# Sliding windows on one core: both windows of one channel half in one copy

## The chip, the cores and the metric

The kernel runs on one core of a Trainium2 chip. The metric is the device time of one execution in microseconds, as the median of several runs.

## The reference

The input is 16 images of 64 channels and 64 x 64 float32 values. Every 8 x 8 window at stride 4 is copied out, 15 x 15 of them an image. Nothing is computed; 16.8 MB are read and 62.9 MB are written.

```python
n_h = (h - window_size) // stride + 1
n_w = (w - window_size) // stride + 1
for i in range(n_h):
    for j in range(n_w):
        result[:, i, j] = x[:, :, i*stride : i*stride + 8, j*stride : j*stride + 8]
```

## The kernel before

**Layout.** Lt holds the whole input in SBUF. A partition is (channel half, image, quarter of the image's rows): 2 x 16 x 4 = 128 partitions, each with 32 channels of 16 rows of 64 values. So partitions 0 to 63 hold the first half of the channels and 64 to 127 the second. A channel takes 1024 values and 32 of padding (PAD). Windows that begin at row 0 or 4 or 8 of a quarter lie within one partition; those that begin at row 12 need the first four rows of the next quarter, which lies on the next partition.

**Output.** One window of one image has 4096 values (16 KB), in the order channel, row, column. A row of windows (15 of them) is cut into 10 lines of 6144 values (24 KB): a line is three halves of a window, numbered n = 0, 1, 2. One half of a window is the 32 channels of one channel half. In a line the channel halves alternate, so n = 0 and n = 2 are of the same channel half in two neighbouring windows, and n = 1 is of the other. `line(k)` lists the three for line k.

**Buffers.** GG has room for three tiles of 24 KB a partition. At the start it is also the staging place for part of the input: the loads at L126 (on the ACT and SP queues) bring some channels there, the copies at L145 move them into Lt, and the loads at L61 (SP and POOL queues) bring the rest directly. The tiles are handed out in a ring: tile t may be filled when the scatter of the tile that had the place before has landed.

**Tiles, in program order.**

- part(y, j), six of them: 16 KB a partition, whole windows for half of the images (y), with four copies of 32 partitions for each channel half (L196), on ACT and DVE by turns. The first three are filled in places of 16 KB, so that a later tile of 24 KB can lie over two of them; and a tile of 24 KB that follows a part tile finds its third n free early.
- plain(k), for k = 4 to 8: a line for windows that begin at rows 0 and 4 of the quarters, rows 0 on the one half of the partitions and rows 4 on the other. Six copies of 64 partitions x 2048 values: three on ACT (L216), and on DVE one written as a shuffle with an identity mask (L154) and two copies (L216).
- cross(k), ten of them: a line for windows that begin at rows 8 and 12. Rows 8 are three copies on ACT (L229). Rows 12 are made on DVE of three shuffles (L154), which bring four rows from the next partition, and three copies (L233), 64 x 1024 values each. Of 128 partitions 16 have no window; their rows' indices are out of bounds and the scatter drops them.
- two edge tiles for the last line of a row: 64 partitions, with copies split over channels between ACT (12 channels) and DVE (20) at L260, and a plain store on the SP queue (L261).

plain(4) to plain(6) alternate with the last three part tiles. Then comes plain(7), cross(0) to cross(4), plain(8), cross(5) to cross(9), and the edges.

**Stores.** All but the edge tiles go out through `scatter` (L162): an indirect DMA issued by POOL, which writes each partition's run to the row of the output that an index tile names (idx for plain, idx_y0 or idx_y1 for part, idx_hi or idx_lo for cross). The index tiles are made once at the start by 21 small operations on DVE. The stores are declared to write rows of their own, so none waits for another. The framework schedules the copies of each engine; only the moves and the part copies keep program order.

## Time and profile before

| | |
|---|---|
| median of 3 runs | 185.22 us (185.2 to 185.27) |
| the profiled execution | 184.96 us, of it 183.2 us span |
| DVE busy | 142.1 us, 183 instructions |
| ACT busy | 140.8 us, 82 instructions |
| POOL busy | 40.0 us, 42 instructions |
| HBM read, written | 16.78 MB, 62.91 MB |

The span runs from the first to the last instruction of the program on the core. A group of instructions is given as line, engine, operation, output <- input, shape and count, then busy us and mean ns of one, then the engine's idle time just before them and what ended it. "DMA out_dram<-GG,idx" as the one that ended an idle time is the landing of a scatter whose tile's place is then free. A queue's share is the time of its packets as a share of 16 DMA engines' span.

### The profile page before, as it was taken

To read this page: it belongs to the slowest core of one execution; us is meant where nothing else is said; L and a number is where in the kernel's file an instruction comes from. 1 tells how busy PE (TensorE), PEld (TensorE's weight loads), DVE (VectorE), ACT (ScalarE), POOL (GpSimd) and SP (SyncE) were. 2 spreads that over 40 slices of the span, in tenths; PEclk is the share of its full clock that TensorE was granted. 3 is DMA by queue.
4 is the path that set the end of the run, shared out by engine and by line. 5 is a ranking of instruction groups with operands and counts; after the bars stand their busy time and mean duration, and the time that the engine had idled before them with its cause. 6 is when DMAs were issued, how large, how long until landed. Compare 5 with 4: busy or idle time off the path is not lost.

```text
span 183.2 us, 516 instructions
## 1 busy us (share of the span) xinstructions
DVE 142.1 (78%) x183; ACT 140.8 (77%) x82; POOL 40.0 (22%) x42
## 2 busy tenths in 40 slices
DVE  4002998999999959979999588979879689986900
ACT  0002998999999969989899488979979789987900
POOL 7500754033330420231112202201220220230000
DMA  4999999999999999999999999999999999999994
GB/s 154 397 413 410 410 410 411 411 412 437 426 440 456 429 395 440 438 429 433 429 453 429 429 431 429 429 435 429 429 429 435 429 431 419 429 429 435 429 429 182
DMA packets 9509, 75.80 MB, mean 414 GB/s; under 512 B 2753, under 2 KB 2753, under 8 KB 6849
## 3 DMA queue, kind: packets, MB, share of 16 engines
q0 software_dynamic: 6736, 62.92, 81.1%
q1 hardware_dynamic: 2192, 10.75, 14.3%
q10 hardware_dynamic: 576, 2.10, 3.1%
q14 instruction: 5, 0.03, 0.0%
HBM read 16.78 MB, written 62.91 MB: 435 GB/s over the span
## 4 chain that ended last, share of the span: by engine, by line
DMA 75%; DVE 11%; POOL 3%; ACT 2%; issue 2%; ACTq 0%; DVEq 0%; PEldq 0%
DMA out_dram<-GG,idx 28%; DMA out_dram<-GG,idx_lo 21%; DMA Lt<-in_x_dram 20%; DVE GG L154 7%; DMA out_dram<-GG,idx_hi 6%; POOL Lt L61 3%; ACT GG L260 2%; DVE GG L233 2%; DVE GG L196 2%; DVE GG L216 1%; ACTq L292 0%; DVEq L154 0%; POOL pi L77 0%; DVEq L216 0%; PEldq L292 0%
## 5 line engine op out<-in xcount | busy, mean ns | idle before, releaser
L229 ACT COPY GG<-Lt 64x2048 f32<-64x2048 f32 x30 | 56.9, 1897 | 9.4 <-DMA out_dram<-GG,idx 4.9
L154 DVE STREAM_SHUFFLE GG<-Lt 64x1024 f32<-64x1024 f32 (+1 forms) x35 | 50.5, 1443 | 0.9
L196 DVE COPY GG<-Lt 32x2048 f32<-32x2048 f32 x30 | 36.6, 1218 | 4.4 <-DMA out_dram<-GG,idx 2.9
L196 ACT COPY GG<-Lt 32x2048 f32<-32x2048 f32 x18 | 34.1, 1897 | 3.0 <-DMA out_dram<-GG,idx 2.1
L216 ACT COPY GG<-Lt 64x2048 f32<-64x2048 f32 x15 | 28.3, 1897 | 1.5 <-DMA out_dram<-GG,idx_lo 1.3
L145 DVE COPY Lt<-GG 32x2048 f32<-32x2048 f32 (+1 forms) x10 | 11.3, 1172 | 13.6 <-DMA GG<-in_x_dram 13.5
L233 DVE COPY GG<-Lt 64x1024 f32<-64x1024 f32 x30 | 20.5, 683 | 0.6
L61 POOL DMA_DIRECT2D Lt<-in_x_dram x16 | 13.9, 878 | 15.8 <-DMA Lt<-in_x_dram 15.3
L162 POOL DMA_INDIRECT out_dram<-GG,idx_y x6 | 9.4, 1573 | 31.5 <-DVE GG L196 27.2
L145 ACT ACT_TABLE_LOAD x1 | 1.3, 1283 | 17.0 <-DMA GG<-in_x_dram 17.0
L216 DVE COPY GG<-Lt 64x2048 f32<-64x2048 f32 x10 | 12.1, 1221 | 0.2
L260 ACT COPY GG<-Lt 32x768 f32<-32x768 f32 x12 | 10.0, 830 | 2.1 <-DMA out_dram<-GG,idx_lo 1.3
L260 DVE COPY GG<-Lt 32x1280 f32<-32x1280 f32 x12 | 9.8, 819 | 2.1 <-DMA out_dram<-GG,idx_lo 1.3
L162 POOL DMA_INDIRECT out_dram<-GG,idx_lo x5 | 4.8, 960 | 29.8 <-DVE GG L233 29.8
L162 POOL DMA_INDIRECT out_dram<-GG,idx_hi x5 | 5.3, 1066 | 26.2 <-DVE GG L233 18.0
L162 POOL DMA_INDIRECT out_dram<-GG,idx x5 | 6.3, 1252 | 20.2 <-ACT GG L216 17.1
L145 ACT COPY Lt<-GG 32x2048 f32<-32x2048 f32 (+1 forms) x6 | 10.3, 1752 | 0.1
L154 DVE LOAD_MASK_SELECT GG<-Lt x35 | 0.3, 8 | 8.7 <-DMA out_dram<-GG,idx 3.8
L80 DVE TENSOR_SCALAR tb<-pi 128x1 int32<-128x1 int32 x1 | 0.2, 154 | 1.0 <-POOL pi L77 1.0
L83 DVE TENSOR_SCALAR tb<-tb 128x1 int32<-128x1 int32 x2 | 0.3, 153 | 0.0
L86 DVE TENSOR_TENSOR th<-tc,tq 128x1 int32<-128x1 int32 x2 | 0.3, 150 | 0.0
L77 POOL IOTA pi<- 128x1 int32 x1 | 0.1, 124 | 0.4 <-PEq L292 0.4
(20 smaller groups left out, 2.9 us busy)
## 6 DMA issues: line engine op xcount, KB each, us to landing
Lt<-in_x_dram POOLq DMA_DIRECT2D x8, 800.0 KB, 16.4
out_dram<-GG SPq DMA_DIRECT2D x2, 1536.0 KB
Lt<-in_x_dram SPq DMA_DIRECT2D x6, 384.0 KB
GG<-in_x_dram ACTq DMA_DIRECT2D x4, 512.0 KB
Lt<-in_x_dram SPq DMA_DIRECT2D x6, 320.0 KB
GG<-in_x_dram SPq DMA_DIRECT2D x4, 448.0 KB
Lt<-in_x_dram SPq DMA_DIRECT2D x2, 704.0 KB
Lt<-in_x_dram POOLq DMA_DIRECT2D x8, 64.0 KB, 16.1
```

The costliest lines, as they stand in the source:

```text
L61: eng.dma_start(out=L[p0 : p0 + QP - HQ + 1 : HQ, c0:c1, :, :], in_=x_v[ch, y, q, :, c0:c1, :])
L80: nc.vector.tensor_scalar(out=d[:, :], in0=pi[:, :], scalar1=shift, scalar2=mask, op0=ALU.logical_shift_right, op1=ALU.bitwise_and)
L83: nc.vector.tensor_scalar(out=d[:, :], in0=a[:, :], scalar1=float(m), scalar2=None, op0=ALU.mult)
L86: nc.vector.tensor_tensor(out=d[:, :], in0=a[:, :], in1=b[:, :], op=op)
L145: tc.keep_in_program_order(copy(out=L[d, c:e, :, :], in_=S[ch][f, c:e]))
L154: nc.vector.stream_shuffle(out=out, in_=in_, mask=mask)
L162: st = nc.gpsimd.indirect_dma_start(out=rows, out_offset=bass.IndirectOffsetOnAxis(ap=ix[:, 0:1], axis=0), in_=g, in_offset=None, element_ ...
L196: (act if n % 3 == 0 else dve)(out=g[d * QP : (d + 1) * QP, ch], in_=L[f : f + QP, :, s * ST : s * ST + WS, cols],)
L216: (copy or (dve if m else shf))(out=g[d, n], in_=L[f, :, half * ST : half * ST + WS, cols])
L229: act(out=g[lo, n], in_=L[f, :, s * ST : s * ST + WS, cols])
L233: dve(out=g[hi, n, :, 0:ST], in_=L[f, :, (s + 1) * ST : RB, cols])
L260: copy(out=g[d, n, c0:c1], in_=L[f, c0:c1, s * ST : s * ST + WS, cols])
```

## The change

In a line, n = 0 and n = 2 are moved by one operation, whose source pattern has one more step (two windows, 4 values apart) and whose destination is two runs of 2048 values with one such run left out between them; n = 1 has an operation of its own. `line(k)` now returns these two groups, and `windows` builds the source pattern. In plain tiles ACT takes the pair of the one row half and the single one of the other, DVE the other two. In cross and edge tiles each engine does what it did, in pairs. Part tiles keep their copies. The index tiles are made in 18 operations; idx_y1 is gone, and the second half of the images is reached by a constant offset of the scatter.

```diff
-    pi, tb, tq, tc_, th, tu, idx, idx_y0, idx_y1, idx_lo, idx_hi = (
+    pi, tb, tq, tc_, te, tu, idx, idx_y, idx_lo, idx_hi = (
...
-    tt(idx_y0, tu, th, ALU.add)
-    nc.vector.tensor_scalar(out=idx_y1[:, :], in0=idx_y0[:, :], scalar1=float(YB * NWIN), scalar2=None, op0=ALU.add)
+    tt(idx_y, tu, tq, ALU.add)
+    far(tb, te, HP + HQ - 1)
+    tt(idx_hi, idx, tb, ALU.add)
+    far(te, te, HQ - 1)
+    line_of(tc_, tc_, -2 * NR, NR)
+    tt(te, te, tc_, ALU.add)
+    tt(idx_lo, idx, te, ALU.add)
...
-        scatter(t, (idx_y0, idx_y1)[y], o_v, j)
+        scatter(t, idx_y, o_v, j + y * YB * NWIN)
...
     def line(k):
-        return [(n, (3 * k + n) % CH, slice((3 * k + n) // CH * ST, (3 * k + n) // CH * ST + WS)) for n in range(3)]
+        j, ch = 3 * k // CH, 3 * k % CH
+        return (j, ch, slice(0, 3, 2), 2), (j + ch, 1 - ch, slice(1, 2), 1)
+
+    def windows(f, c, r, j, m):
+        v = L[f, c, r, j * ST : j * ST + WS]
+        return bass.AP(tensor=v.tensor, offset=v.offset, ap=[v.ap[0], [ST, m], *v.ap[1:]])
...
     def plain(k):
         t = tile_()
         g = halves(t, 3)
-        work = [(half, n, ch, cols) for half in range(CH) for n, ch, cols in line(k)]
-        for copy, ops in ((act, work[::2]), (None, work[1::2])):
-            for m, (half, n, ch, cols) in enumerate(ops):
+        for half in range(CH):
+            for j, ch, n, m in line(k):
                 f = slice(ch * HP, (ch + 1) * HP)
                 d = slice(half * HP, (half + 1) * HP)
-                (copy or (dve if m else shf))(out=g[d, n], in_=L[f, :, half * ST : half * ST + WS, cols])
+                copy = (shf if m == 1 else act) if half == 0 else (dve if m == 2 else act)
+                copy(out=g[d, n], in_=windows(f, every, slice(half * ST, half * ST + WS), j, m))
         scatter(t, idx, o_l, k)
...
-        for n, ch, cols in line(k):
+        for j, ch, n, m in line(k):
             f = slice(ch * HP, (ch + 1) * HP)
-            act(out=g[lo, n], in_=L[f, :, s * ST : s * ST + WS, cols])
-            shf(out=g[hi, n, :, ST:WS], in_=L[f, :, 0:ST, cols], mask=nxt)
-        for n, ch, cols in line(k):
+            act(out=g[lo, n], in_=windows(f, every, slice(s * ST, s * ST + WS), j, m))
+            shf(out=g[hi, n, :, ST:WS], in_=windows(f, every, slice(0, ST), j, m), mask=nxt)
+        for j, ch, n, m in line(k):
             f = slice(ch * HP, (ch + 1) * HP)
-            dve(out=g[hi, n, :, 0:ST], in_=L[f, :, (s + 1) * ST : RB, cols])
+            dve(out=g[hi, n, :, 0:ST], in_=windows(f, every, slice((s + 1) * ST, RB), j, m))
...
-        for n, ch, cols in line(NR - 1):
+        for j, ch, n, m in line(NR - 1):
...
                 for c0, c1, copy in ((0, ACT_C, act), (ACT_C, CL, dve)):
-                    copy(out=g[d, n, c0:c1], in_=L[f, c0:c1, s * ST : s * ST + WS, cols])
+                    copy(out=g[d, n, c0:c1], in_=windows(f, slice(c0, c1), slice(s * ST, s * ST + WS), j, m))
```

More of the change, by code (lines that the diff above doesn't have):

```diff
@@ L66, in itile @@
         return ipool.tile([P, 1], i32, name=name)
-    pi, tb, tq, tc_, th, tu, idx, idx_y0, idx_y1, idx_lo, idx_hi = (
-        itile(n) for n in ("pi", "tb", "tq", "tc", "th", "tu", "idx", "idx_y0", "idx_y1", "idx_lo", "idx_hi")
+    pi, tb, tq, tc_, te, tu, idx, idx_y, idx_lo, idx_hi = (
+        itile(n) for n in ("pi", "tb", "tq", "tc", "te", "tu", "idx", "idx_y", "idx_lo", "idx_hi")
     )
@@ L86, in tt, with line_of, far @@
         nc.vector.tensor_tensor(out=d[:, :], in0=a[:, :], in1=b[:, :], op=op)
+    def line_of(d, a, mult, add):
+        nc.vector.tensor_scalar(out=d[:, :], in0=a[:, :], scalar1=float(mult), scalar2=float(add), op0=ALU.mult, op1=ALU.add)
+    def far(d, a, value):
+        nc.vector.tensor_scalar(out=d[:, :], in0=a[:, :], scalar1=float(value), scalar2=FAR, op0=ALU.is_equal, op1=ALU.mult)
     bits(tb, 2, B - 1)
-    bits(tq, 0, HQ - 1)
+    nc.vector.tensor_scalar(out=tq[:, :], in0=pi[:, :], scalar1=2, scalar2=NSLOT * (HQ - 1), op0=ALU.logical_shift_left, op1=ALU.bitwise_and)
     bits(tc_, 6, 1)
+    bits(te, 0, HP + HQ - 1)
     mul(tb, tb, NH)
-    mul(th, tq, NSLOT)
-    tt(tb, tb, th, ALU.add)
+    tt(tb, tb, tq, ALU.add)
     tt(tu, tb, tc_, ALU.add)
     mul(idx, tu, NR)
-    bits(th, 5, 1)
-    mul(th, th, 1 - YB * NWIN)
+    bits(tq, 5, 1)
+    mul(tq, tq, 1 - YB * NWIN)
     mul(tu, tu, NW)
-    tt(idx_y0, tu, th, ALU.add)
-    nc.vector.tensor_scalar(out=idx_y1[:, :], in0=idx_y0[:, :], scalar1=float(YB * NWIN), scalar2=None, op0=ALU.add)
-    nc.vector.tensor_scalar(out=tq[:, :], in0=tq[:, :], scalar1=float(HQ - 1), scalar2=FAR, op0=ALU.is_equal, op1=ALU.mult)
-    tt(th, tc_, tq, ALU.mult)
-    tt(idx_hi, idx, th, ALU.add)
-    nc.vector.tensor_scalar(out=tc_[:, :], in0=tc_[:, :], scalar1=-1.0, scalar2=1.0, op0=ALU.mult, op1=ALU.add)
-    tt(tb, tb, tc_, ALU.add)
-    mul(tb, tb, NR)
-    tt(th, tc_, tq, ALU.mult)
-    tt(idx_lo, tb, th, ALU.add)
+    tt(idx_y, tu, tq, ALU.add)
[5 more added lines that the diff above has]
+    tt(idx_lo, idx, te, ALU.add)
     NG = 3
@@ L200, in part @@
             )
-        scatter(t, (idx_y0, idx_y1)[y], o_v, j)
+        scatter(t, idx_y, o_v, j + y * YB * NWIN)
     def line(k):
-        return [(n, (3 * k + n) % CH, slice((3 * k + n) // CH * ST, (3 * k + n) // CH * ST + WS)) for n in range(3)]
+        j, ch = 3 * k // CH, 3 * k % CH
[3 more added lines that the diff above has]
+        return bass.AP(tensor=v.tensor, offset=v.offset, ap=[v.ap[0], [ST, m], *v.ap[1:]])
+    every = slice(0, CL)
     crossed = 0
```

## The prediction

> **What bounds the kernel now.** I read the page's header, its slices and its queues first, then busy time by stage, then the groups of instructions by shape, then the waits, and last the order of time on VectorE (DVE), ScalarE (ACT) and GpSimd (POOL) where one tile hands over to the next.

> ```profile
> span 183.2 us, 516 instructions
> DVE 142.1 (78%) x183; ACT 140.8 (77%) x82; POOL 40.0 (22%) x42
> DMA  4999999999999999999999999999999999999994
> q0 software_dynamic: 6736, 62.92, 81.1%
> q1 hardware_dynamic: 2192, 10.75, 14.3%
> q10 hardware_dynamic: 576, 2.10, 3.1%
> HBM read 16.78 MB, written 62.91 MB: 435 GB/s over the span
> ```

> The three DMA queues together took 81.1 + 14.3 + 3.1 = 98.5% of 16 engines' span. Only the first and the last of 40 slices are not full. DVE and ACT have 41 us each in which they do nothing. The stages say the same more closely (columns: window, its length, busy time of DVE, ACT and POOL, clock, DMA share, GB/s):

> ```profile
> 1.00:2.00 1.00, 0.96 (x11) 0.00 (x0) 0.51 (x1) 1.00 0.00 0
> 2.00:3.00 1.00, 0.86 (x9) 0.00 (x0) 1.00 (x3) 1.00 0.71 127
> 44.00:92.00 48.00, 44.01 (x40) 44.66 (x25) 11.22 (x9) 1.00 1.01 432
> 92.00:162.00 70.00, 60.26 (x90) 59.90 (x32) 9.77 (x11) 1.00 1.01 432
> 64.00:68.00 4.00, 2.09 (x2) 2.53 (x2) 0.96 (x1) 1.00 0.92 395
> 180.00:181.00 1.00, 0.00 (x0) 0.00 (x0) 0.00 (x0) 1.00 0.63 270
> ```

> The first bytes move between 2.0 and 2.3 us (0.71 of a microsecond is filled), the last in about 180.6. Between them the share is 1.0 or over in both long stages and the rate is 432 GB/s in both, although DVE and ACT are 92% busy in the one (44.01 of 48) and 86% in the other. A rate that does not follow how busy the engines are is the rate of the transfers themselves. The weakest stretch in them is 64 to 68, at 0.92: 4 x 0.08 = 0.3 us of traffic lost at most. So the kernel is a stream of transfers with about 2 us ahead of it and 2.6 us behind its last bytes, and a copy on DVE or ACT counts only where it leaves that stream without work.

> How far off that is, the scatters show:

> ```profile
> DMA to landing us min/median/max: 9.9/12.5/15.0
> 59.66 1.85 POOL L162 DMA_INDIRECT out_dram<-GG,idx_y  x1 [4.40 <-DVE GG L196]
> 65.89 0.96 POOL L162 DMA_INDIRECT out_dram<-GG,idx  x1 [4.38 <-ACT GG L216]
> 78.96 1.54 POOL L162 DMA_INDIRECT out_dram<-GG,idx  x1 [3.66 <-ACT GG L216]
> 86.14 0.96 POOL L162 DMA_INDIRECT out_dram<-GG,idx_y  x1 [5.63 <-DVE GG L196]
> 91.20 0.96 POOL L162 DMA_INDIRECT out_dram<-GG,idx  x1 [4.11 <-ACT GG L216]
> 91.29 9.59 ACT L229 COPY GG<-Lt 64x2048 f32<-64x2048 f32 x5 [0.77 <-DMA out_dram<-GG,idx]
> 98.00 12.46 DMA out_dram<-GG,idx_lo
> ```

> A line tile is 128 rows of 24 KB, 3.15 MB, or 7.3 us at 432 GB/s; a part tile is 2.10 MB, 4.9 us; a cross tile drops 16 rows, 2.75 MB, 6.4 us. From issue to landing a scatter takes 9.9 to 15.0 us, so it always waits behind another. The shortest cover is at plain(6): issued at 78.96, and the ACT copy at 91.29 is let go by its landing. Of these 12.3 us, 7.3 are its own traffic, 1.54 POOL's work on it, and about 1.5 the way from an issue to the first bytes (my estimate, from the load issues that begin at 0.74, row below, to the first bytes by 2.3). That leaves 2.0 us of waiting behind other traffic, less the receipt, for which the rows give only a bound: 183.2 - 181 = 2.2 us at the end of the kernel. The real cover there is thus between nothing and 2.0 us. For cross(0), 12.46 - 6.4 - 0.96 - 1.5 = 3.6 us, less the same receipt. I take the middle: 1 us at the tightest hand-over, and 3.6 - 1.1 = 2.5 us in the cross stage.

> ```profile
> 0.74 2.61 ACTq L126 DMA_DIRECT2D GG<-in_x_dram  x4
> ```

> **The change, part by part.** The rows for its costs:

> ```profile
> L229 ACT COPY GG<-Lt 64x2048 f32<-64x2048 f32 x30 | 56.9, 1897 | 9.4 <-DMA out_dram<-GG,idx 4.9
> L154 DVE STREAM_SHUFFLE GG<-Lt 64x1024 f32<-64x1024 f32 x30 | 38.4, 1280 | 0.7
> L233 DVE COPY GG<-Lt 64x1024 f32<-64x1024 f32 x30 | 20.5, 683 | 0.6
> L154 DVE STREAM_SHUFFLE GG<-Lt 64x2048 f32<-64x2048 f32 x5 | 12.1, 2427 | 0.2
> L216 DVE COPY GG<-Lt 64x2048 f32<-64x2048 f32 x10 | 12.1, 1221 | 0.2
> L260 ACT COPY GG<-Lt 32x768 f32<-32x768 f32 x12 | 10.0, 830 | 2.1 <-DMA out_dram<-GG,idx_lo 1.3
> L260 DVE COPY GG<-Lt 32x1280 f32<-32x1280 f32 x12 | 9.8, 819 | 2.1 <-DMA out_dram<-GG,idx_lo 1.3
> L145 ACT COPY Lt<-GG 32x1024 f32<-32x1024 f32 x1 | 1.0, 1036 | 0.0
> L145 DVE COPY Lt<-GG 32x2048 f32<-32x2048 f32 x9 | 10.7, 1227 | 13.6 <-DMA GG<-in_x_dram 13.5
> ```

> Durations. ACT: 2048 elements in 1897 ns and 1024 in 1036 make 0.841 ns an element and 175 ns of fixed cost, so one of 4096 is 3.62 us. DVE copy: 1221 and 683 ns make 0.525 ns an element and 146 fixed, so 4096 is 2.30 us. The merged shuffle of a cross tile is 64x2048, which a row has: 2.43 us in place of 2 x 1.28.

> Plain tiles (5). ACT had 3 copies, 5.7 us; it gets one of 4096 and one of 2048, 5.5. DVE had a shuffle and two copies, 2.43 + 2 x 1.22 = 4.9; it gets a shuffle and one copy of 4096, 4.7. The split between the engines stays; each tile is ready 0.2 us sooner.

> Cross tiles (10). ACT as above, 5.7 to 5.5 us. DVE: 3 x 1.28 + 3 x 0.68 = 5.9 becomes 2.43 + 1.28 + 1.22 + 0.68 = 5.6.

> Edge tiles (2). Six operations an engine become four. ACT: 6 x 0.83 = 5.0; two of 1536 elements at 1.47 and two of 768 at 0.83 make 4.6. DVE: 6 x 0.82 = 4.9; two of 2560 at 1.49 and two of 1280 at 0.82 make 4.6.

> Sum of busy time. ACT loses 5 + 10 + 4 = 19 operations of 175 ns, 3.3 us. DVE loses 5 + 10 + 4 = 19 copies of 146 ns and 10 shuffles of 133 (2 x 1280 - 2427), 4.1 us. All of it lies beside transfers: the share is 1.0 wherever these copies run. On the path it is worth nothing. If the cover were gone, it would be worth at most 5 x 0.2 + 10 x 0.3 + 2 x 0.3 = 4.6 us, which is also what the change would have brought to a kernel bound by its copies.

> What is no longer done early. This is the one place where the change takes something away. A line tile that takes a buffer after a part tile (16 of 24 KB) had its third window column, n = 2, free before the rest. The order on DVE shows such pieces run ahead of their tile:

> ```profile
> 63.89 1.22 DVE L216 COPY GG<-Lt 64x2048 f32<-64x2048 f32 x1
> 85.40 1.29 DVE L154 STREAM_SHUFFLE GG<-Lt 64x1024 f32<-64x1024 f32 x1
> 90.34 0.69 DVE L233 COPY GG<-Lt 64x1024 f32<-64x1024 f32 x1
> 79.16 6.21 DVE L196 COPY GG<-Lt 32x2048 f32<-32x2048 f32 x5 [0.97 <-DMA out_dram<-GG,idx]
> ```

> The 64x1024 shuffle at 85.40 and the copy at 90.34 belong to a cross tile, while plain(7) is still being filled (its scatter goes out at 91.20). An operation over n = 0 and n = 2 must wait for both. For plain(6), plain(7) and cross(1) up to one ACT copy (1.90 us) and 1.2 to 2.0 us of DVE then move behind the landing. But the pieces run ahead stood in front of the tile that was due: without them plain(5) and plain(7) go out 1.2 to 2.0 us sooner. In this stage tiles wait for engines more than for landings (DVE 44.01 of 48 us busy), so for plain(6) and plain(7) it cancels. Only cross(1) comes later, by about 1.3 us, behind cross(0), whose traffic still fills 6.4 us. Cost on the path: nothing; bounds 0 and +1.3 - 1 = +0.3 us if the cover there is as thin as at plain(6).

> Waits. Each merged operation waits for all the landings that its two halves waited for. Behind it on ACT stands the other copy of the tile, on DVE the rest of it, and the scatter on POOL waits for both. The two halves of an operation lie on either side of n = 1, which the other engine writes in a plain tile; if the two were ordered one after the other, ACT's 3.62 and then DVE's 2.43 make 6.05 against 5.74 now: +0.3 a tile, within the cover.

> Index tiles. 3 of 21 operations on 128x1 go, 0.15 us each:

> ```profile
> L101 DVE TENSOR_SCALAR idx_y<-idx_y 128x1 int32<-128x1 int32 x1 | 0.2, 154 | 0.0
> ```

> 0.45 us of DVE at the start, on an engine that next waits 13.5 us for the staged loads (L145's row above). Nothing. idx_y1 goes because the second half of the batch is now a constant offset of the scatter; rows and bytes stay.

> Descriptors. No DMA is added or moved past another. But POOL's work on a scatter depends on what DVE runs beside it: 0.96 us at 86.14 beside shuffles, 1.85 at 59.66 beside 1.22 us copies. The second has 0.89 us more than the first, 0.73 of such a copy. The copy beside it in a plain tile will be one of 2.30 us. The bounds are 0.96 (never in its way) and 0.96 + 2.30 = 3.3 us (a whole copy), so -0.9 to +1.4 against the 1.85 of now, at the three part scatters that go out beside plain copies (59.66, 73.98, 86.14); I take the same share of the longer copy, 0.96 + 0.73 x 2.30 = 2.6 us, +0.8, and it is covered: even the shortest flight, 9.9 us, has 9.9 - 4.9 - 0.96 - 1.5 = 2.5 us behind other traffic, less the receipt. [...]

> **Sum.** 0 on the path. The profiled execution took 184.96 us, 1.8 around a span of 183.2; the median of the runs is 185.22, 0.26 above it. 184.96 + 0 + 0.26 = 185.2 us.

> **Rivals.** What this kernel's measurement can tell from no change is about 0.2%, 0.37 us.

> A, slower: late descriptors. POOL's longer wait beside the longer copies costs the stream its cover in the part stage. It decides once a scatter is late by more than the cover of 1 us: +1.4 at each of three, less 1, is +0.4 a tile, +1.2 in all: 186.4. For: 1.85 against 0.96, and the part stage has DVE 92% busy. Against: a part scatter has 2.5 us behind other traffic where plain(6) has 2.0, and plain(6)'s 1.54 passed without a dip. Chance 0.12.

> B, slower: DVE loses half its rate on the new pattern. [...] Against: L145 keeps the full rate (1227 ns) with a stride in both operands. Chance 0.05. [...]

> C, slower: order. A merged 3.62 us copy placed ahead of a tile that is due delays it by 1.7 us more than a single one; less 1, +0.7: 185.9. Chance 0.03.

> D, faster. The 0.3 us of dip at 64 to 68, and others as small, close because tiles come 0.2 to 1.2 us sooner: 184.7. Against: at 64 to 68 the scatter issued at 59.66 was already waiting, so lateness is not what made it. Chance 0.10.

> E, the merged operations are taken apart again when the program is lowered: counts as now, 185.2. It lies within no change.

> **The numbers.** No change, E included, 0.70; A, B and C make slower 0.20; D faster 0.10. The range goes from D, 184.7, to A, 186.4, and leaves out B and part of D, under 1 in 10 with the far ends of A.

> **What would show it.** Right: 19 fewer ACT copies, 15 of them 64x4096 at 3.6 us; 5 DVE copies of 64x4096 at 2.3; 15 shuffles of 64x2048 and 10 of 64x1024; both engines 3 to 4 us less busy and idle for longer behind landings; 432 GB/s from 44 to 162. Wrong: a DMA share under 0.92 in any 4 us between 44 and 176, POOL over 2.5 us on a scatter, a DVE copy near 4.7 us, or a span that moves by over 0.4 us with the stream still full.

## The result and the profile after

The changed kernel takes 184.71 us in the median of 14 runs (184.51 to 185.06); the kernel before took 185.15 us in 14 runs beside it (184.97 to 185.27). The ratio is 0.9977 [0.997, 0.9984], so 0.44 us or 0.23% less. That is within the range of 184.7 to 186.4, but just past the 0.2% that the forecast of "no change" allowed, on the side that it gave a chance of 0.1. The profiled execution took 184.68 us, 1.8 around a span of 182.9.

The page's header and queues after, with the line that names the fourth queue, which the prediction did not weigh:

```profile
span 182.9 us, 453 instructions
DVE 138.7 (76%) x141; ACT 137.5 (75%) x63; POOL 40.4 (22%) x42
DMA  4999999999999999999999999999999999999995
q0 software_dynamic: 6736, 62.92, 81.3%
q1 hardware_dynamic: 2192, 10.75, 14.3%
q10 hardware_dynamic: 576, 2.10, 3.1%
q14 instruction: 3, 0.02, 0.0%
HBM read 16.78 MB, written 62.91 MB: 436 GB/s over the span
```

The fourth queue in the kernel before:

```profile
q14 instruction: 5, 0.03, 0.0%
```

DVE has lost 3.4 us and ACT 3.3 (142.1 and 140.8 before). POOL has 0.4 more. The queues take 81.3 + 14.3 + 3.1 = 98.7% of the span where they took 98.5%: the same traffic in a span that is 0.3 us shorter. The stages of the changed kernel (columns as before):

```profile
44.00:92.00 48.00, 41.61 (x33) 42.22 (x20) 10.93 (x9) 1.00 1.01 432
92.00:162.00 70.00, 60.62 (x63) 60.14 (x23) 9.69 (x11) 1.00 1.01 431
64.00:68.00 4.00, 1.57 (x2) 2.30 (x2) 0.96 (x1) 1.00 0.92 395
180.00:181.00 1.00, 0.00 (x0) 0.00 (x0) 0.00 (x0) 1.00 0.52 221
181.00:182.00 1.00, 0.00 (x0) 0.00 (x0) 0.00 (x0) 1.00 0.01 0
```

The rate is what it was, 432 and 431 GB/s against 432 twice. The dip from 64 to 68 is there unchanged, 0.92 and 395 GB/s. Nothing in the stream has become denser. Only the end differs: from 180 to 181 a share of 0.52 where there was 0.63. This view counts a packet's whole time where the packet starts. The packet records show when the last one ends: at 181.89 us before and at 181.61 after. So the last bytes do not stop at about 180.6, as the prediction read the view, and 1.3 us of the span lie behind them in both kernels, not 2.6. Its forecast does not hang on this.

The groups by shape, the merged operations first:

```profile
L238 ACT COPY GG<-Lt 64x4096 f32<-64x4096 f32 x10 | 36.0, 3603 | 8.4 <-DMA out_dram<-GG,idx_lo 4.6 <-DMA out_dram<-GG,idx 3.3 <-DMA out_dram<-GG,idx_hi 0.3
L225 ACT COPY GG<-Lt 64x4096 f32<-64x4096 f32 x5 | 18.0, 3604 | 3.7 <-DMA out_dram<-GG,idx_y 2.1 <-DMA out_dram<-GG,idx_lo 1.5
L225 DVE COPY GG<-Lt 64x4096 f32<-64x4096 f32 x5 | 11.4, 2289 | 0.2
L155 DVE STREAM_SHUFFLE GG<-Lt 64x2048 f32<-64x2048 f32 x15 | 36.4, 2428 | 0.3
L155 DVE STREAM_SHUFFLE GG<-Lt 64x1024 f32<-64x1024 f32 x10 | 12.8, 1280 | 0.3
L269 ACT COPY GG<-Lt 32x1536 f32<-32x1536 f32 x4 | 5.9, 1469 | 2.6 <-DMA out_dram<-GG,idx_lo 2.4 <-DMA out_dram<-GG,idx_hi 0.2
L269 DVE COPY GG<-Lt 32x2560 f32<-32x2560 f32 x4 | 5.9, 1486 | 2.4 <-DMA out_dram<-GG,idx_lo 2.3
```

15 ACT copies of 64x4096 at 3603 and 3604 ns (3.62 us was worked out), 5 on DVE at 2289 (2.30), 15 shuffles of 64x2048 at 2428 (2.43), and the edge copies at 1469 and 1486 (1.47 and 1.49). So the copies did what the prediction said.

The scatters that the prediction named (start, length, what ended POOL's idle time):

```profile
48.62 2.39 POOL L163 DMA_INDIRECT out_dram<-GG,idx_y  x1 [4.36 <-DVE GG L197]
59.64 0.97 POOL L163 DMA_INDIRECT out_dram<-GG,idx_y  x1 [4.40 <-DVE GG L197]
74.08 0.96 POOL L163 DMA_INDIRECT out_dram<-GG,idx_y  x1 [7.43 <-DVE GG L197]
78.88 1.69 POOL L163 DMA_INDIRECT out_dram<-GG,idx  x1 [3.84 <-ACT GG L225]
86.19 0.96 POOL L163 DMA_INDIRECT out_dram<-GG,idx_y  x1 [5.63 <-DVE GG L197]
103.54 0.96 POOL L163 DMA_INDIRECT out_dram<-GG,idx_hi  x1 [4.74 <-issue]
162.47 2.39 POOL L163 DMA_INDIRECT out_dram<-GG,idx_hi  x1 [6.05 <-ACT GG L238]
```

### The profile page after: what moved, and what is told of

Its sections match the earlier page's. It is cut to its first block, busy times and chain, and to the rows that moved or that the text cites. A ratio compares the mean times of both kernels' runs of the same rounds, so it can differ in the third digit from the quotient of the medians.

```text
span 182.9 us, 453 instructions
## 1 busy us (share of the span) xinstructions
DVE 138.7 (76%) x141; ACT 137.5 (75%) x63; POOL 40.4 (22%) x42
## 3 DMA queue, kind: packets, MB, share of 16 engines
q0 software_dynamic: 6736, 62.92, 81.3%
q1 hardware_dynamic: 2192, 10.75, 14.3%
HBM read 16.78 MB, written 62.91 MB: 436 GB/s over the span
## 4 chain that ended last, share of the span: by engine, by line
DMA 75%; DVE 13%; POOL 3%; issue 2%; DVEq 1%; POOLq 0%; PEldq 0%
DMA out_dram<-GG,idx 28%; DMA out_dram<-GG,idx_lo 21%; DMA Lt<-in_x_dram 20%; DMA out_dram<-GG,idx_hi 6%; DVE GG L155 6%; POOL Lt L61 3%; DVE GG L242 2%; DVE GG L197 2%; DVE GG L269 2%; DVE GG L225 1%; DVEq L301 1%; POOL pi L77 0%; DVEq L155 0%; POOLq L163 0%; DVEq L269 0%
## 5 line engine op out<-in xcount | busy, mean ns | idle before, releaser
L238 ACT COPY GG<-Lt 64x4096 f32<-64x4096 f32 (+1 forms) x20 | 55.0, 2750 | 8.6 <-DMA out_dram<-GG,idx_lo 4.6
L155 DVE STREAM_SHUFFLE GG<-Lt 64x2048 f32<-64x2048 f32 (+1 forms) x25 | 49.2, 1969 | 0.6
L197 ACT COPY GG<-Lt 32x2048 f32<-32x2048 f32 x18 | 34.1, 1897 | 4.0 <-DMA out_dram<-GG,idx 2.8
L225 ACT COPY GG<-Lt 64x4096 f32<-64x4096 f32 (+1 forms) x10 | 27.5, 2750 | 3.8 <-DMA out_dram<-GG,idx_y 2.1
L242 DVE COPY GG<-Lt 64x2048 f32<-64x2048 f32 (+1 forms) x20 | 19.1, 955 | 0.5
L163 POOL DMA_INDIRECT out_dram<-GG,idx_y x6 | 8.8, 1474 | 31.8 <-DVE GG L197 31.8
L163 POOL DMA_INDIRECT out_dram<-GG,idx_hi x5 | 6.2, 1248 | 28.7 <-DVE GG L242 17.9
L225 DVE COPY GG<-Lt 64x4096 f32<-64x4096 f32 x5 | 11.4, 2289 | 0.2
L269 ACT COPY GG<-Lt 32x1536 f32<-32x1536 f32 (+1 forms) x8 | 9.2, 1150 | 2.7 <-DMA out_dram<-GG,idx_lo 2.4
L269 DVE COPY GG<-Lt 32x2560 f32<-32x2560 f32 (+1 forms) x8 | 9.2, 1152 | 2.5 <-DMA out_dram<-GG,idx_lo 2.3
L163 POOL DMA_INDIRECT out_dram<-GG,idx x5 | 6.4, 1283 | 20.5 <-ACT GG L225 18.2
```

Of the source, the lines that this page charges most:

```text
L155: nc.vector.stream_shuffle(out=out, in_=in_, mask=mask)
L163: st = nc.gpsimd.indirect_dma_start(out=rows, out_offset=bass.IndirectOffsetOnAxis(ap=ix[:, 0:1], axis=0), in_=g, in_offset=None, element_ ...
L197: (act if n % 3 == 0 else dve)(out=g[d * QP : (d + 1) * QP, ch], in_=L[f : f + QP, :, s * ST : s * ST + WS, cols],)
L225: copy(out=g[d, n], in_=windows(f, every, slice(half * ST, half * ST + WS), j, m))
L238: act(out=g[lo, n], in_=windows(f, every, slice(s * ST, s * ST + WS), j, m))
L242: dve(out=g[hi, n, :, 0:ST], in_=windows(f, every, slice((s + 1) * ST, RB), j, m))
```

## The experiments

Each edit is against the kernel before, or against the changed one where it says so. Each kernel was run 5 to 12 times beside 24 to 33 runs of the kernel before, whose median was 185.09 to 185.13 us; differences are against that median.

### One part at a time

**Index tiles alone.** The kernel before, with the 18 index operations of the change and the constant offset in the scatter; the copies stay single.

```diff
-    pi, tb, tq, tc_, th, tu, idx, idx_y0, idx_y1, idx_lo, idx_hi = (
+    pi, tb, tq, tc_, te, tu, idx, idx_y, idx_lo, idx_hi = (
...
-        scatter(t, (idx_y0, idx_y1)[y], o_v, j)
+        scatter(t, idx_y, o_v, j + y * YB * NWIN)
```

> The kernel before with only the index tiles in 18 operations and idx_y with the constant offset. Theory F (the stream of transfers is full from 2 to 180 us; only what its two ends look like can count): 0.0 us, as DVE waits 13.5 us for the staged loads after them; at most -0.1 us. Theory I (fewer small operations and a shorter program at the start let the first loads move sooner): -0.3 to -0.4 us, the whole gain.

The result, -0.33 us, is the number of theory I, but its mechanism did not show: the first packet starts at 2.18 us with and without the edit.

**Copies alone.** All merged copies, with the 21 index operations of before.

```diff
-            act(out=g[lo, n], in_=L[f, :, s * ST : s * ST + WS, cols])
+            act(out=g[lo, n], in_=windows(f, every, slice(s * ST, s * ST + WS), j, m))
...
-                    copy(out=g[d, n, c0:c1], in_=L[f, c0:c1, s * ST : s * ST + WS, cols])
+                    copy(out=g[d, n, c0:c1], in_=windows(f, slice(c0, c1), slice(s * ST, s * ST + WS), j, m))
```

> The changed kernel with the 21 index operations of before: all the merged copies and nothing else. Theory F: -0.3 to -0.45 us, the whole gain, all of it after 143 us. Theory I: 0.0 us.

**Edges alone** has only the second of these two edits (the edge tiles), **lines alone** only the first with its like in plain and cross.

> Only the two edge tiles have merged copies; all else as before. Theory E (the gain is the tail: the edge stores go out sooner, and the last packets end more evenly): -0.3 to -0.4 us; the SP stores go out about 0.4 us sooner than 167.6 and 173.9. Theory C (the gain is in the line tiles: scatters go out 0.2 to 0.3 us sooner and the stream has fewer thin places): 0.0 us.

> Only the plain and cross tiles have merged copies; edges and index tiles as before. Theory C: -0.3 to -0.4 us. Theory E: 0.0 us, or up to -0.1 as the place of the first edge tile is filled a little sooner.

| kernel | median, us | ratio to before | difference, us |
|---|---|---|---|
| index tiles alone | 184.80 | 0.9986 [0.9977, 0.9995] | -0.33 |
| copies alone | 184.99 | 0.9995 [0.9986, 1.0004] | -0.14 (not told from 0) |
| edges alone | 185.14 | 1.0 [0.9991, 1.0009] | 0.0 |
| lines alone | 185.45 | 1.002 [1.0011, 1.0029] | +0.32 |

Two things follow. First, most of the gain belongs to the index tiles, which the prediction had set at nothing; index and copies together make -0.47, and the whole change -0.44. Second, the copies don't add up: edges are worth nothing and lines cost 0.32, but both together cost nothing (-0.14, with an interval that holds 0). So merging the edges is worth 0.46 on top of the lines and nothing without them. Busy time would add. That looks like something with a threshold.

**Before again and after again** are the two kernels as they are.

> The kernel before once more, against itself: 0.0 us. How far its ratio is from 1, and how far the ends of its 16 DMA engines lie apart in its profile (179.3 to 181.9 us for the last packets in the first profile), says how much of the differences of 0.1 to 0.3 us is chance.

> The changed kernel once more: -0.44 us if its gain is its own. Theory S (the transfers' sum is the same, and what differs is by how many 0.91 us packets the slowest of the 16 DMA engines ends behind the others): the mean end of the engines within 0.1 us of the kernel before, the last end 0.2 to 0.4 us sooner. Theory C (scatters that go out sooner close thin places in the stream): the mean end itself is 0.3 us sooner.

They gave 185.13 us, 1.0001 [0.9992, 1.001], and 184.63 us, 0.9977 [0.9968, 0.9986]. So the gain is there a second time, and what these runs can tell apart is about 0.1%. In the two profiles the engines' last packets end on the mean at 180.99 us (before again) and 180.94 (after again), and the very last at 181.91 and 181.56. That is as theory S had it, not theory C.

### Is it one operation of 0.15 us, or the cover?

**Offset alone.** The kernel before without the one operation that made idx_y1, 20 in place of 21. The tile idx_y1 goes with it, and a constant offset in the scatter takes its place.

```diff
...
-    nc.vector.tensor_scalar(out=idx_y1[:, :], in0=idx_y0[:, :], scalar1=float(YB * NWIN), scalar2=None, op0=ALU.add)
...
-        scatter(t, (idx_y0, idx_y1)[y], o_v, j)
+        scatter(t, idx_y0, o_v, j + y * YB * NWIN)
```

> The kernel before with the constant offset of the scatter in place of idx_y1: 20 index operations. If the offset is what made the 18-operation kernel 0.33 us faster: -0.3 us. If it is the number of operations at the start: -0.1 us. If it is chance in how the engines end (theory S): anything within 0.3 us of the kernel before.

It gave 184.78 us, 0.9982 [0.9973, 0.9991], -0.34 us. This one edit does all that the index part does; the other two operations are worth nothing that shows. It removes 0.15 us of DVE at a time when DVE then idles for 13.5 us, so it isn't DVE's time that comes back. Which of the three things in the edit counts (the operation, the tile's place, the offset) it does not tell; the tile's place is tried below.

**Slower cross tiles.** The changed kernel, with part of the copies in each of the ten cross tiles made twice: 64x512 values more on DVE and 64x512 more on ACT.

```diff
             dve(out=g[hi, n, :, 0:ST], in_=windows(f, every, slice((s + 1) * ST, RB), j, m))
+            if m == 1:
+                dve(out=g[hi, n, 0 : CL // 2, 0:ST], in_=windows(f, slice(0, CL // 2), slice((s + 1) * ST, RB), j, m))
+                act(out=g[lo, n, 0 : CL // 4], in_=windows(f, slice(0, CL // 4), slice(s * ST, s * ST + WS), j, m))
```

> The changed kernel, and in each of the 10 cross tiles a part of its copies is made twice: 64x512 more on DVE (0.41 us) and 64x512 more on ACT (0.61 us), so that DVE is 4 us and ACT 6 us busier, more than the change saved. Theory F (the stream is full, copies are covered): within 0.3 us of the changed kernel. A kernel bound by its copies in the cross stage: +4 to +6 us.

It gave 185.29 us, 1.0011 [1.0002, 1.002], 0.6 us above the changed kernel. This kernel's page shows how much busy time was added:

```profile
DVE 142.9 (78%) x151; ACT 143.6 (78%) x73; POOL 40.5 (22%) x42
```

That is 4.2 us of DVE and 6.1 of ACT more than the changed kernel has, and the kernel is 0.6 us slower. That is more than the 0.3 us of theory F, and far from the 4 to 6 us of a kernel bound by its copies. So nearly all of the cover that the prediction assumed is there; that copies cheaper by 3.4 us should have gained 0.44 is not likely. What the 0.6 goes with stands below.

### The place of the buffer

One index tile less also moves the buffer GG in SBUF: the tiles take 32 bytes a partition each, and GG lies behind them, at byte 152032 before and at 152000, a multiple of 64, with ten tiles. These bytes follow from how the program lays out its tiles; no view of the profile shows an address. I took the place for the cause, and tested it by a wider tile `pi` that pushes GG on:

```diff
-        return ipool.tile([P, 1], i32, name=name)
+        return ipool.tile([P, 16 if name == "pi" else 1], i32, name=name)[:, 0:1]
```

| kernel | GG at byte | ratio to before | median, us |
|---|---|---|---|
| before | 152032 | 1 | 185.09 |
| offset alone, GG put back | 152032 | 0.9985 [0.9977, 0.9994] | 184.84 |
| after, GG put back | 152032 | 0.9973 [0.9962, 0.9983] | 184.65 |
| before, moved | 152064 | 0.998 [0.9971, 0.9989] | 184.78 |
| after, moved (24 in place of 16) | 152064 | 0.9941 [0.9929, 0.9954] | 184.12 |

**Offset alone, GG put back.**

> The kernel with the constant offset alone (-0.34 us), but GG put back to byte 152032. Theory P: 0.0 us, the gain is gone. Theory O: -0.34 us still.

**After, GG put back.**

> The changed kernel with GG put back to byte 152032. Theory P: -0.12 us, what the merged copies are worth by themselves (the kernel with them and the old index tiles gave -0.14). Theory O: -0.44 us as the changed kernel.

**Before, moved.**

> The kernel before, all 21 index operations and idx_y1 kept, but one index tile 32 bytes wider, so that GG begins 32 bytes later in each partition: at byte 152064, a multiple of 64, where it began at 152032, which is not; with 10 index tiles it begins at 152000, a multiple of 64 too. Theory P (what idx_y1's removal brought is GG's place): -0.34 us, as much as the constant offset alone. Theory O (the offset or the operation itself): 0.0 us.

**After, moved.**

> The changed kernel with GG at byte 152064, a multiple of 256, where it is at 152000, a multiple of 64 only. Theory P with 64 bytes as the unit: -0.44 us as the changed kernel. If larger units count: sooner still, -0.6 to -0.8 us. Theory O: -0.44 us.

My theory fell: with GG back at the old byte the gain stays, 0.25 us of 0.34 and 0.44 of 0.44, and both intervals lie clear of 0. But byte 152064 has a gain of its own, 0.31 us on the kernel before and about 0.5 on the changed one. The kernel that has both takes 184.12 us in 5 runs, 0.5 to 0.6% less than before, and is the best of all that were run. Where that gain lies, the stage after the first cross tiles and the end show. First the kernel before and the changed one, then before moved, then after moved:

```profile
97.00:162.00 65.00, 55.37 (x83) 54.95 (x30) 9.60 (x10) 1.00 1.00 430
97.00:162.00 65.00, 55.68 (x58) 55.19 (x21) 9.63 (x10) 1.00 1.00 430
```

```profile
97.00:162.00 65.00, 55.19 (x82) 54.77 (x29) 9.64 (x10) 1.00 1.01 432
180.00:181.00 1.00, 0.00 (x0) 0.00 (x0) 0.00 (x0) 1.00 0.12 49
```

```profile
97.00:162.00 65.00, 55.72 (x57) 55.06 (x21) 9.64 (x10) 1.00 1.01 432
180.00:181.00 1.00, 0.00 (x0) 0.00 (x0) 0.00 (x0) 1.00 0.07 25
```

432 GB/s in place of 430, with the engines equally busy, and few packets still start after 180 (a share of 0.12 and 0.07, where it was 0.63 and 0.52). The last packets end on the mean at 180.60 and 180.39 us, where they ended at 181.06 and 181.00.

In the packet records, the mean of the 1888 packets of 24 KB is 915.1 ns before and 914.9 after, but 913.1 and 912.7 in the two moved kernels; the other ten profiles have 914.8 to 916.1. About 118 of them on each of 16 engines make 118 x 2.0 = 0.24 us of the 0.31, and 118 x 2.2 = 0.26 of the 0.5. The difference is not spread over all packets. From 44 to 97 us the 24 KB packets take 912.6 ns in the kernel before and 912.6 in before moved, and the 16 KB packets of part tiles, from the same buffer, 611 to 612 in all four. Nearly all of the difference comes later: 917.8 against 914.0 ns from 125 to 162 us, and 916.3 against 912.8 after that, where 142 packets take 920 ns or more before and 46 when moved. So the place of the buffer changes how many packets run long in the last third, and why is open.

## Why the prediction was right and where it was wrong

**Copies, durations, sum of busy time: right but for one size.** Every duration came within 0.02 us, and ACT lost the 3.3 us that were worked out. DVE lost 3.4 where 4.1 were worked out for its copies and shuffles and 0.45 for the index operations. The term that was too large is the fixed cost. plain(8) on DVE, before and after (start, length):

```profile
125.81 2.36 DVE L216 COPY GG<-Lt 64x2048 f32<-64x2048 f32 x2
```

```profile
125.76 2.29 DVE L225 COPY GG<-Lt 64x4096 f32<-64x4096 f32 x1
```

Two copies of 1.22 us in a row took 2.36 together, one of twice the size takes 2.29. The second of the two begins at 126.95, 0.08 us before the first ends (125.81 + 1.22 = 127.03), so one less brings 0.07 us here, not 146 ns. None of it shows as time, as the prediction said (copies alone can't be told from 0), and slower cross tiles show it from the other side.

**What is no longer done early: right where it costs, wrong where it gains.** cross(1)'s scatter goes out at 103.54 instead of 102.04, 1.5 us later (1.3 was forecast), and no dip follows. plain(5) and plain(7) were to go out 1.2 to 2.0 us sooner. They go at 65.68 and 91.10, 0.2 and 0.1 us sooner, and both wait for ACT. cross(1) before, then plain(5) and plain(7) after:

```profile
102.04 0.96 POOL L162 DMA_INDIRECT out_dram<-GG,idx_hi  x1 [3.08 <-issue]
```

```profile
65.68 0.96 POOL L163 DMA_INDIRECT out_dram<-GG,idx  x1 [5.07 <-ACT GG L225]
91.10 0.96 POOL L163 DMA_INDIRECT out_dram<-GG,idx  x1 [3.95 <-ACT GG L225]
```

**Descriptors: the sign was wrong at two places of three, and nothing hung on it.** The scatters at 59.64 and 74.08 have 0.97 and 0.96 us, not 2.6: DVE now runs the shuffle beside them, not the copy. The third, at 86.19, keeps its 0.96. A long wait showed elsewhere, at 48.62:

```profile
47.88 2.29 DVE L225 COPY GG<-Lt 64x4096 f32<-64x4096 f32 x1
50.20 2.41 DVE L155 STREAM_SHUFFLE GG<-Lt 64x2048 f32<-64x2048 f32 x1
```

POOL begins at 48.62 and takes 2.39 us, to 51.01; the 2.29 us copy beside it ends at 50.17, and 0.84 us later POOL is done, where a scatter beside a shuffle takes 0.96. By these times nearly all of POOL's work at this scatter came after the copy. It cost nothing; rival A did not happen. The same place before:

```profile
48.57 1.74 POOL L162 DMA_INDIRECT out_dram<-GG,idx_y  x1 [4.36 <-ACT GG L216]
```

**Rivals.** D was right in sign and wrong in cause: it had dips close, and the dip from 64 to 68 did not change. B, half rate, would have shown near 4.7 us on the DVE copy, by estimate: 4096 values at the shuffles' 1.12 ns each (from 1280 ns for 1024 and 2427 for 2048), and 0.15 us fixed. It took 2.29; no run shows the half rate. C had a long ACT copy delay a tile that is due; no 4 us from 44 to 176 fall under the share of 0.92 that the kernel before has, too. E had the merged operations taken apart; the rows have them whole. 184.71 us lies within the range by luck: its lower edge came from D's dips, which did not close.

**Index tiles, "Nothing": the step that failed.** It is worth 0.33 us, three quarters of the gain. The working was sound on DVE's time and weighed nothing else that goes with an instruction.

**What goes with the gain.** The fourth queue of the page, q14, has the kind "instruction", and it has 5 packets in the kernel before and 3 in the changed one. I read those of 8 KB that come while the kernel runs as fetches of pieces of the program; the traces show the kind, the times and the sizes. Its rows in the queue view, for windows of a few microseconds; first the kernel before, from 39 to 42, beside the other queue that runs then:

```profile
q0 software_dynamic: 328, 0.67, 57.2%
q14 instruction: 1, 0.01, 0.7%
```

the changed kernel, from 45 to 48 (it has no such row from 39 to 42, nor from 144 to 182):

```profile
q0 software_dynamic: 77, 1.26, 98.9%
q14 instruction: 1, 0.01, 0.6%
```

and lines alone, from 170 to 182, while the edge tiles are stored:

```profile
q1 hardware_dynamic: 159, 3.15, 61.3%
q14 instruction: 1, 0.01, 0.2%
```

A piece is one packet of 8 KB that takes 309 ns in the full stream (333 ns at 40.6 us, during the loads). It costs the engine that carries it more than that, since the packet behind it also runs long: 1260 to 1266 ns in place of 912 for the fetches from 148 us on. The two late ones, of lines alone and slower cross, have a long packet ahead of them as well (1168 and 1164 ns). With 912 ns taken as a packet's own time, that makes 256 + 309 + 350 = 0.92 us on one engine in lines alone, and 0.91 in slower cross. The times of the later fetches go with the number of instructions on the page: with 508 to 516 of them the second comes at 71.2 to 71.6 us, with 453 to 464 at 82.5 to 82.9, and there the last comes at 173.5 with 464, 177.8 with 463, 183.3 with 456 and 184.0 with 453. The last columns come from the packet records: the mean time at which the last 16 packets of 24 KB end, about one for each DMA engine, and when the very last one ends.

| kernel | median, us | fetches at, us | mean end | last end |
|---|---|---|---|---|
| before | 185.15 | 40.6, 71.4, 106.6, 148.5 | 181.06 | 181.89 |
| edges alone | 185.14 | 40.6, 71.6, 106.8, 147.8 | 181.21 | 182.08 |
| index tiles alone | 184.80 | 46.9, 71.5, 106.7, 148.3 | 180.97 | 181.74 |
| offset alone | 184.78 | 45.7, 71.2, 106.6, 148.4 | 180.92 | 181.77 |
| copies alone | 184.99 | 40.5, 82.6, 107.4, 183.3 | 180.95 | 181.49 |
| after | 184.71 | 47.1, 82.9, 107.7, 184.0 | 181.00 | 181.61 |
| lines alone | 185.45 | 40.7, 82.5, 107.5, 173.5 | 181.05 | 182.35 |
| slower cross | 185.29 | 46.8, 82.6, 107.6, 177.8 | 181.18 | 182.07 |

The mean end is 180.9 to 181.2 in all eight: the traffic as a whole takes the same time. The stream ends with the slowest of 16 DMA engines, 0.5 to 1.3 us after the mean, and there the kernels differ.

- The last fetch. Copies alone and after have three fetches before the stream's end and the fourth behind it (183.3, 184.0), where it harms nothing; their last end is 0.54 and 0.61 us after the mean. Before, edges and index have it at 148, and 0.77 to 0.87. Lines alone has it at 173.5, in the last 10 us, and 1.30: it ends last and is the slowest of all. Slower cross has it at 177.8 and is 0.6 us slower than after. An engine's packets follow each other within some 5 ns (in the kernel before, 96% of the packets of 4 KB and more that start from 140 to 179 us do so within 5 ns of another's end), so the one that carried the fetch can be followed to the end. In slower cross it is the engine that ends last, at 182.07. In lines alone it is, too, at 182.35, if the long packet is the one behind the fetch, as elsewhere, and near ties are taken in order. This fits a threshold: with the edges merged too, the last piece comes when the stream is done.
- The first fetch. All kernels in which idx_y1's operation is gone have it at 45.7 to 47.1; all that have that operation have it at 40.3 to 40.8, while the last loads are on their way. Index tiles alone and offset alone, in which little else differs from before, gain 0.33 and 0.34.
- In numbers, against before: the first fetch moved, -0.33; the last behind the end, -0.14 (not told from 0); the last in the final 10 us, +0.3 (lines alone) and, from after, +0.6.

**What is shown and what is not.** Shown by runs: that the constant offset in place of idx_y1's operation is worth 0.34 us, that GG's byte is not what brings it, that the index part without any cheaper copy brings most of the gain, and that merging edges pays only together with lines. Read from the traces is that the times of the fetches go with the gains in the twelve profiles whose GG is not moved to byte 152064; before moved gains 0.31 with its fetches where they were (40.3 and 148.3). That the fetches cause the gains was not tried by itself: no kernel was run that has the same work and only a fetch moved.

For a last fetch in the final 10 us the traces show the price and the place: 0.9 us on one engine, which then ends last (in slower cross, and by the likeliest order in lines alone). For the first fetch they don't, and speak rather against it. The packet behind it takes 492 ns in place of 159 at 40.6 us, and 1036 in place of 611 at 46.9 (index tiles alone), so its engine loses 0.67 us in the one and 0.73 in the other. Nor do the profiles show the gain of 0.33. The profiled executions took 184.96 and 184.98 us before, 184.81 with index tiles alone and 184.84 with offset alone. The profiles before are at the low end of their kernel's runs, and the one of copies alone, with 184.74, lies 0.25 us under its median. So differences of 0.1 to 0.2 us in the columns on the right mean nothing. Why removing idx_y1's operation brings 0.34 us in the median stays open.

## What to carry to other kernels

Where a stream of transfers is full, as here, cheaper copies hardly move the mean end of the DMA engines (180.9 to 181.2 us), and what is left to win is a few tenths of a microsecond: look at the page's instruction queue, at when its packets come, and at the byte at which a large buffer starts, before counting engine time. A part that costs "nothing" by its engine's time is still so many instructions and so many bytes of SBUF, so where 0.2% matters, run it alone. When parts don't add up (0 and +0.32 made -0.14 here), look for a threshold, not for a sum. And where a few tenths of a microsecond count, compare the profiled execution with the median before reading a cause from its trace.
